# A table of relative biases, spread through a DRAM tape: 16 copies of its rows in place of 128, and eight read-backs in place of one

## The chip, the cores and the metric

The kernel runs on one core of a Trainium2 chip. The metric is the device time of one execution in microseconds (us); lower is better. The engines are TensorE (PE, with its weight loads shown as PEld), VectorE (DVE), ScalarE (ACT), GpSimd (POOL) and SyncE (SP). Each has its own queue of instructions and runs it in order. Transfers are issued by SP (the weights), by POOL (small inputs, and the table of this case) and once by ACT, and run on 16 DMA engines.

## The reference

Two blocks of a network on x of shape (1, 512, 1024), all in fp32. The first is a SwiGLU feed-forward layer, a mixer (chunked attention with 8 heads of 64, beside a pooling of trailing means), and a second feed-forward layer, with RMS norms and residuals. The second block has differential attention, an mLSTM and an MLP. The part that the change touches is the bias of the chunked attention, which depends on the distance of query and key alone, clipped at 128:

```python
x = x + 0.5 * swiglu_ffn(rmsnorm(x, ffn1_norm[l]), ...)
x = x + hybrid_mixer(rmsnorm(x, mix_norm[l]), ...)      # holds chunked_attention
x = x + 0.5 * swiglu_ffn(rmsnorm(x, ffn2_norm[l]), ...)

# chunked_attention: each chunk of 64 attends to itself and the 8 before it
rel_idx = jnp.clip(qpos - kpos, -REL_CLIP, REL_CLIP) + REL_CLIP
bias = rel_bias.astype(jnp.float32)[:, rel_idx]          # rel_bias: (8 heads, 257)
s = jnp.einsum('bhqd,bhkd->bhqk', qb, kb).astype(jnp.float32) * scale + bias
s = jnp.where(valid[None, None], s, NEG_INF)
p = jax.nn.softmax(s, axis=-1)
```

## The kernel before, in words

**Tiles.** Activations stand with features on 128 partitions and the 512 tokens in the columns. Every fp32 operand is split into a high and a low part of a shorter type, and each product is three matmuls (high x high, high x low, low x high). A weight tile of 128 x 1024 words is loaded by SP into one of 3 buffers `wraw`; ScalarE copies its high part to `whi` and VectorE subtracts to get `wlo`, each with 4 buffers. The load of the third tile on is issued when a tile has been split. One weight tile feeds 24 matmuls of 512 columns in the feed-forward layer.

**The first feed-forward layer (`ffn`).** It goes in three chunks of 8, 8 and 6 blocks of 128 hidden features. For each block there are a gate and an up product into two banks; VectorE multiplies both by the norm's scale, ScalarE takes silu of the gate, POOL multiplies the two, and ScalarE and VectorE split the result into its two parts for the down product at the end of the chunk. Behind the second chunk two side jobs are noted: `late_cols` and `toeplitz`.

**The bias table (`toeplitz`).** The biases of the 256 nearest distances, less that of the farthest, are turned around with two small transposes and two small matmuls into a row `rv` of 384 words for each of 8 heads, of which the first 128 are zero. POOL then issues a write of these rows, repeated, to a DRAM tile, the tape, and reads it back with a stride that is one word shorter than a row, so that each partition gets the row shifted by one more word: a table with the same value along each diagonal, `te[128, 8, 512]`, in the memory that held x (`XT`). A POOL memset then masks a part of it (partitions 0 to 63, 64 columns of each head). The table is read by VectorE in the score step of the mixer (`soft_unit`).

**Order.** Nothing is issued as it is written. `Program.note` records each instruction with its operands, a price in ns and, for a transfer, a landing time; `Program.issue` then runs a list schedule in 60 sweeps forwards and backwards, with a little random noise on the ranks (one draw for each noted instruction in each sweep, from a fixed seed), keeps the shortest plan and issues each engine's queue in its order. The first block, up to the end of the mixer, is planned in one go, and the rest in a second. All instructions thus have the line of the issuing loop, 232, and are told apart by their tiles. Of a transfer the planner takes:

```python
if "dma" in fn:
    op.dma = max(math.prod(outs[0].shape) / 90.0, 300.0)
    op.lag = 1900.0 + op.dma
...
if "dma" in fn:
    return {"POOL": 1000.0}.get(eng, 60.0)
```

Of the kernel before, what the change touches and what calls it, by code (L numbers as in the profile page):

```python
# [9 lines left out]
F32 = mybir.dt.float32  # L10
# [5 lines left out]
P = 128  # L16
S = 512
H2 = 256
# [36 lines left out]
class Engine:  # L55
    """Stands for an engine's queue: what is called on it is noted, not issued."""
# [8 lines left out]
class Program:  # L65
    """Notes the instructions in the order of the data flow, then issues each engine's in the order of a list schedule:
    of those whose operands are there, one early in the program or with a long path behind it goes first."""
# [12 lines left out]
    @staticmethod  # L80
    def boxes(aps):
        """(tile, first and end partition, first and end column) of each run."""
        out = []
        for ap in aps:
            t = ap.tensor
            if not isinstance(t, tile.Tile):
                continue
            dims = list(ap.ap)
            if ap.space == bass.MemoryType.DRAM:
                out.append((t.name, 0, 1, 0, 1))  # L90
                continue
            row, parts = dims.pop(0)
            p0, f0 = divmod(ap.offset, row)
            runs = [f0]
            while len(dims) > 1 and len(runs) * dims[0][1] <= 32:
                s, c = dims.pop(0)
                runs = [f + s * i for f in runs for i in range(c)]
            n = sum(s * (c - 1) for s, c in dims) + 1
            out += [(t.name, p0, p0 + parts, f, f + n) for f in runs]
        return out  # L100
# [29 lines left out]
    def edge(self, a, b, flow=True):  # L130
        """b after a; flow: b reads what a writes."""
        if a.dma:
            lat = 60.0
        elif a.eng == b.eng and not flow:
            lat = 0.0
        else:
            lat = SIGNAL[a.eng][b.eng]
        if a.i < self.first:
            b.floor = max(b.floor, a.end + lat)
        else:  # L140
            a.succ[b.i] = max(a.succ.get(b.i, 0.0), lat)

    def table(self, name):
        """Loads a set of function tables, after every use of the one before it."""
        op = self.add("ACT", self.engines[2].queue.preload_act_table_set, (name,), {}, 1290.0)
        for u in self.users + [self.load] * (self.load is not None):
            self.edge(u, op)
        self.load, self.users = op, []
# [30 lines left out]
    @staticmethod  # L179
    def cost(eng, fn, outs, ins, k):  # L180
        """Nanoseconds that the instruction holds its engine."""
        n = max(math.prod(x.shape[1:]) for x in outs[:1] + ins[:1])
        psum = any(x.space == bass.MemoryType.PSUM for x in outs[:1] + ins)
        if "dma" in fn:
            return {"POOL": 1000.0}.get(eng, 60.0)
        if eng == "PE":
            n = math.prod(outs[0].shape[1:])
            if fn == "transpose":
                return max(0.855 * n, 13.0)
            return max(n, 256) / 2.4 + 3 if k["rhs"].dtype == F32R else max(1.667 * n, 214.0)  # L190
        cols = sum(1 for x in ins if math.prod(x.shape[1:]) == 1 and n > 1)
        if eng == "ACT":
            return 0.834 * n + (51.0 if psum else 93.0) + 93.0 * (cols + (k.get("accum_out") is not None))
        if eng == "POOL":
            return 2.11 * n + 147.0 if fn == "tensor_tensor" else 0.83 * n + 200.0
        big = [x for x in ins if math.prod(x.shape[1:]) > 1]
        if len(big) <= 1 and not psum:
            return 0.52 * n + 65.0 + 61.0 * cols
        return 1.041 * n + 69.0 + 61.0 * cols

# [1 line left out]
    def issue(self):  # L202
        """Issues what was noted since the last time. Sweeps forwards and backwards in turn, each by the times of the one
        before with a little noise, and the shortest counts."""
        first, ops = self.first, self.ops[self.first:]
        after = [[(j - first, lat) for j, lat in op.succ.items()] for op in ops]
        before = [[] for _ in ops]
# [27 lines left out]
    def sweep(self, ops, nexts, needs, rank, back):  # L235
# [8 lines left out]
        while n < len(ops):  # L244
# [11 lines left out]
            # one that comes soon and is more urgent is waited for  # L256
# [21 lines left out]
class Arena:  # L278
    """Memory of the phases, cut from one tile for each type."""
# [35 lines left out]
class Kern:  # L315
# [22 lines left out]
    def turn(self, b, blocks):  # L338
        """Transposes of blocks of 128 columns, side by side."""
        for i, x in enumerate(blocks):  # L340
            self.pe.transpose(b[:, i * P:(i + 1) * P], x, self.ident)

    def split(self, h, l, src, g=None):
        """Two parts of src (times the column g) that hold all its bits."""
        if g is None:
            self.act(h, src, AF.Copy)
            self.tt(l, src, h.bitcast(F32), ALU.subtract)
        else:
            self.act(h, src, AF.Copy, scale=g)
            self.stt(l, src, g, h.bitcast(F32), ALU.mult, ALU.subtract)  # L350

    def rsqrt(self, v, n, y, t):
        """y = v ** -0.5 on [128, n] columns."""
        v, y, t = v[:, :n], y[:, :n], t[:, :n]
        self.ts(y.bitcast(I32), v.bitcast(I32), -0.5, ALU.mult, 1597463007.0, ALU.add)
        for _ in range(3):
            self.tt(t, y, y, ALU.mult)
            self.stt(t, t, -0.5, v, ALU.mult, ALU.mult)
            self.stt(y, t, 1.5, y, ALU.add, ALU.mult)

# [112 lines left out]
    def fgroup(self, ps, w, xs, c0=0, cols=slice(0, S)):  # L473
        """Features on partitions: the weights stay, the tokens move."""
        wh, wl = w
        n = len(xs)
        for k in range(n):
            self.mm3(ps, wh[:, k, c0:c0 + P], wl[:, k, c0:c0 + P], xs[k][0][:, cols], xs[k][1][:, cols],
                     k == 0, k == n - 1)

    def fgroups(self, bs, ws, xs, cols=slice(0, S)):
        """The same for several banks, step by step."""
# [5 lines left out]
    def tstep(self, b, w, xs, t, k, start, stop, cols=slice(0, S)):  # L488
        """Tokens on partitions: block t's share of the k-th rows."""
# [16 lines left out]
    def sum_parts(self, b, src, mat, eps, n=S):  # L506
        """b = mat.T @ (src + eps), src in two exact parts."""
# [6 lines left out]
    def rs_wide(self, b, n, y, t, eng=None):  # L514
        """y = (b / n) ** -0.5: a seed from the tables, then a Newton step."""
# [18 lines left out]
    def norm(self):  # L534
        """rsb[:, t] = rms(x[t]) ** -1 on every partition."""
# [4 lines left out]
    def to_cols(self, b, dst, src):  # L540
        """One row of src as a column for each block of tokens."""
# [8 lines left out]
    def setup(self):  # L550
# [6 lines left out]
        self.tape = dp.tile([8, P, 384], F32, name="tape")  # L557
# [63 lines left out]
    def first_norm(self):  # L621
        tb = Rot(self.B[4:8])
        # the clock of the tensor engine rises while it is busy
# [25 lines left out]
    def toeplitz(self, T):  # L649
        """T[q, h, 512 - w + s] = bias of a key s of w, less that of the farthest; later chunks masked."""  # L650
# [14 lines left out]
        self.po.dma_start(self.tape, rv.unsqueeze(1).to_broadcast([8, P, 384]))  # L665
# [3 lines left out]
        self.po.dma_start(te[:, :, H2:], bass.AP(src.tensor, src.offset + P, [[383, P], [384 * P, 8], [1, H2]]))  # L669
        self.po.memset(te[0:64, :, 448:512], NEG)  # L670

# [37 lines left out]
    def stack_q(self, dst, src, half, g=None):  # L709
        """dst = [high part; low part] of the 64 rows of src in the given half."""  # L710
# [8 lines left out]
    def stack_k(self, kh, kl, src, half, g=None):  # L719
        """kh, kl = the high part of the 64 rows, twice, and the low part."""  # L720
# [4 lines left out]
    def qk_mm(self, out, a, b, half):  # L725
        """Of stacked operands (one of them a q, the other kh and kl)."""
# [18 lines left out]
    def transposes(self, E, PT, PL=None):  # L745
        """The blocks of E turned into PT[s, t] for each block of keys."""
# [149 lines left out]
    def prep_final(self, m):  # L896
        """Operands of the second block's first product, and both sums of squares."""
# [12 lines left out]
    def norm_final(self):  # L910
        """The two norms in a row: rsb and rcol for both, X scaled by the first."""
# [26 lines left out]
    def diff_phase(self):  # L938
        I = self.I
        with self.mem.scope() as T:  # L940
# [25 lines left out]
            # gate weights  # L966
# [39 lines left out]
            # lambda  # L1006
# [63 lines left out]
    def gates(self, gs, one, g8):  # L1070
        """Rows of the mLSTM's gates: log of the forget gate, stabiliser, sums within blocks of keys."""
# [144 lines left out]
    def mlp_phase(self):  # L1216
        I = self.I
        X, y = self.X, self.y
        with self.mem.scope() as T:
# [19 lines left out]
            # last part of the mixer's product, then its norm and the residual, by halves of the tokens  # L1239
# [39 lines left out]
            def post(t, cs_, b, part):  # L1279
                """Adds the last part, squares for the norm, and the gain."""  # L1280
# [35 lines left out]
            for t in range(NT):  # L1316
# [9 lines left out]
                # rsqrt(v + eps) of the product's mean square v: a seed from the tables, then a Newton step  # L1326
# [81 lines left out]
```

## Time and profile before

| | |
|---|---|
| median of 3 timed runs | 1563.83 us (1563.27 to 1564.39) |
| profiled execution, first to last instruction | 1561.2 us |
| median less that span | 2.6 us |
| mean granted TensorE clock | 0.993 of full speed |
| TensorE busy | 1531.9 us, 98% of the span |
| VectorE, ScalarE, POOL busy | 53%, 41%, 19% |
| DMA | 142.06 MB, mean 91 GB/s |

The profile gives the span of the profiled execution; no other total stands beside it. A busy share is the part of the span in which an engine works; matmuls are pipelined, so a slow matmul also counts as busy. The granted clock is TensorE's clock as a share of full speed: 1.00 is 2.4 GHz and 0.50 is 1.2 GHz. An arrow in a row names what released the waiting engine last. Names of tiles are written without buffer numbers; `a1f` and `a1r` are the common memory of the first block, of plain fp32 and of split operands.

### The profile page before, as it was taken

The numbers are of one execution on the slowest core, as the hardware profiler recorded it, in microseconds if no ns is written. First come the engines' busy times: TensorE is split into PE (matmuls) and PEld (weight loads), VectorE is DVE, ScalarE is ACT, GpSimd is POOL, SyncE is SP. The second block draws the span as 40 slices with busy tenths as digits, with TensorE's granted clock in tenths as the row PEclk, the third lists the DMA queues.
The fourth block names the chain that finished last, engine by engine and source line by source line (L and its number), as shares of the span: only waits on it lengthen the run. The fifth ranks groups of instructions, "written<-read, shape, count | busy, mean of one in ns | idle before, by whom it ended". The sixth has DMA issues, their size and how long they took to land.

```text
span 1561.2 us, 17985 instructions
## 1 busy us (share of the span) xinstructions
PE 1531.9 (98%) x6931; PEld 1238.2 (79%) x6931; DVE 827.3 (53%) x1284; ACT 647.8 (41%) x1063; POOL 295.4 (19%) x283
## 2 busy tenths in 40 slices
PE   9999999979999999999999999999999999999997
PEld 7888888868867788888888887677778888888886
DVE  6453343335588895433433457988568524344345
ACT  6321231224347763322322355876555534233232
POOL 5120110012054340100200137321106000000002
PEclk9999999989999999999999999999999999999999
DMA  6333333453321114333433233121321332322321
GB/s 190 95 98 93 96 103 96 90 123 108 95 68 50 59 55 122 94 94 95 125 88 102 81 97 101 51 82 32 92 82 44 122 94 90 100 94 94 95 94 54
DMA packets 227237, 142.06 MB, mean 91 GB/s; under 512 B 5524, under 2 KB 212976, under 8 KB 227152
## 3 DMA queue, kind: packets, MB, share of 16 engines
q1 hardware_dynamic: 224832, 136.33, 29.5%
q0 software_dynamic: 2304, 4.59, 1.8%
q8 instruction: 54, 0.88, 0.2%
q14 instruction: 31, 0.25, 0.1%
q10 hardware_dynamic: 16, 0.00, 0.0%
HBM read 137.23 MB, written 3.67 MB: 90 GB/s over the span
## 4 chain that ended last, share of the span: by engine, by line
PE 85%; DVE 6%; issue 3%; DMA 3%; ACT 1%; POOL 1%; SPq 0%; DVEq 0%; POOLq 0%; ACTq 0%
PE bank L232 85%; DMA wraw<-ffn_w_gate 2%; DVE a2f L232 1%; DVE wlo L232 1%; DVE X L232 1%; DVE sq L232 1%; ACT a2f L232 1%; DVE a1r L232 1%; DVE xl L232 0%; POOL a1f L232 0%; DVE a2r L232 0%; DVE XT L232 0%; DMA XT<-x 0%; ACT whi L232 0%; DVE cv L232 0%
## 5 line engine op out<-in xcount | busy, mean ns | idle before, releaser
L232 DVE TENSOR_TENSOR wlo<-wraw,whi 128x1024 fp32r<-128x1024 f32 (+2 forms) x258 | 325.8, 1264 | 449.3 <-ACT whi L232 399.7
L232 ACT ACTIVATE whi<-wraw 128x1024 fp32r<-128x1024 f32 (+2 forms) x258 | 267.3, 1039 | 535.9 <-PE bank L232 493.4
L232 PE MATMUL bank<-xh,whi 128*128 128x512 f32 (+1 forms) x1272 | 464.2, 386 | 10.2 <-ACT whi L232 8.2
L232 PE MATMUL bank<-xl,whi 128*128 128x512 f32 (+1 forms) x1272 | 463.3, 385 | 2.5 <-DVE xl L232 2.5
L232 PE MATMUL bank<-xh,wlo 128*128 128x512 f32 (+1 forms) x1272 | 461.2, 385 | 0.0
L232 PEld LDWEIGHTS bank<-xh,whi 128*128 128x128 f32 x1272 | 239.8, 190 | 59.7 <-ACT whi L232 9.4
L232 PEld LDWEIGHTS bank<-xl,whi 128*128 128x128 f32 x1272 | 240.4, 190 | 50.0 <-DVE xl L232 3.0
L232 PEld LDWEIGHTS bank<-xh,wlo 128*128 128x128 f32 x1272 | 239.8, 190 | 47.5 <-issue 1.4
L232 PE MATMUL bank<-whi,a2r 128*128 128x512 f32 (+1 forms) x528 | 155.6, 388 | 0.0
L232 PE MATMUL bank<-a1r,whi 128*128 128x512 f32 x480 | 149.1, 398 | 0.0
L232 PE MATMUL bank<-a2r,whi 128*128 128x512 f32 x416 | 130.0, 397 | 0.0
L232 PEld LDWEIGHTS bank<-whi,a2r 128*128 128x128 f32 x528 | 98.3, 188 | 21.0
L232 POOL TENSOR_TENSOR a2f<-a2f 128x512 f32<-128x512 f32 x38 | 56.4, 1484 | 303.6 <-DVE a2f L232 252.4
L232 POOL TENSOR_TENSOR a1f<-a1f 128x512 f32<-128x512 f32 x40 | 59.4, 1485 | 248.2 <-DVE a1f L232 234.2
L232 PEld LDWEIGHTS bank<-a1r,whi 128*128 128x128 f32 x480 | 89.3, 188 | 21.5 <-issue 0.6
L232 PE MATMUL bank<-wlo,a2r 128*128 128x512 f32 (+1 forms) x264 | 95.0, 389 | 0.0
L232 PEld LDWEIGHTS bank<-a2r,whi 128*128 128x128 f32 x416 | 77.3, 187 | 19.0 <-issue 0.7
L232 PE MATMUL bank<-a1r,wlo 128*128 128x512 f32 x240 | 91.3, 400 | 0.0
L232 ACT ACTIVATE a2r<-a2f 128x512 fp32r<-128x512 f32 (+3 forms) x83 | 51.0, 620 | 93.1 <-POOL a2f L232 55.3
L232 DVE TENSOR_TENSOR a2r<-a2f,a2r 128x512 fp32r<-128x512 f32 (+2 forms) x81 | 54.8, 679 | 49.7 <-ACT a2r L232 48.9
L232 PE MATMUL bank<-a2r,wlo 128*128 128x512 f32 x208 | 79.4, 397 | 0.0
L232 POOL TENSOR_TENSOR X<-X,a2f 128x512 f32<-128x512 f32 (+1 forms) x9 | 10.7, 1212 | 337.6 <-ACT a2f L232 337.6
(246 smaller groups left out, 1585.7 us busy)
## 6 DMA issues: line engine op xcount, KB each, us to landing
wraw<-ffn_w_gate SPq DMA_DIRECT2D x43, 512.0 KB, 3.7
wraw<-ffn_w_up SPq DMA_DIRECT2D x43, 512.0 KB, 3.7
wraw<-w_in SPq DMA_DIRECT2D x40, 512.0 KB, 3.8
wraw<-ffn_w_down SPq DMA_DIRECT2D x32, 512.0 KB, 3.9
wraw<-w_up SPq DMA_DIRECT2D x32, 512.0 KB, 4.0
wraw<-w_down SPq DMA_DIRECT2D x32, 512.0 KB, 3.6
wraw<-w_out SPq DMA_DIRECT2D x16, 512.0 KB, 3.4
wraw<-ffn_w_down SPq DMA_DIRECT2D x16, 384.0 KB, 3.4
```

The lines of the kernel that those rows point to most:

```text
L232: op.fn(*op.a, **op.k)
```

## The change

The tape holds each head's row 16 times in place of 128 times. One shifted read of it can then fill 16 partitions only, so the read-back is done in eight transfers of 16 partitions each, each starting 16 words earlier in the row than the one before. The rest of the computation is the same. The file after also lacks the comments and docstrings of the one before, with empty lines in their place.

```diff
-        self.tape = dp.tile([8, P, 384], F32, name="tape")
+        self.tape = dp.tile([8, 16, 384], F32, name="tape")
...
-        self.po.dma_start(self.tape, rv.unsqueeze(1).to_broadcast([8, P, 384]))
+        self.po.dma_start(self.tape, rv.unsqueeze(1).to_broadcast([8, 16, 384]))
         self.T = te = self.XT[:].rearrange("p t d -> p (t d)").rearrange("p (h c) -> p h c", h=8)
         self.po.memset(te[:, :, :H2], 0.0)
         src = self.tape[:]
-        self.po.dma_start(te[:, :, H2:], bass.AP(src.tensor, src.offset + P, [[383, P], [384 * P, 8], [1, H2]]))
+        for a in range(8):
+            self.po.dma_start(te[16 * a:16 * a + 16, :, H2:],
+                              bass.AP(src.tensor, src.offset + P - 16 * a, [[383, 16], [384 * 16, 8], [1, H2]]))
         self.po.memset(te[0:64, :, 448:512], NEG)
```

## Rows read from the trace of the kernel before

**Rows 1.** The page: span, busy time, and two lines of the 40 slices (tenths).

```profile
span 1561.2 us, 17985 instructions
...
PE 1531.9 (98%) x6931; PEld 1238.2 (79%) x6931; DVE 827.3 (53%) x1284; ACT 647.8 (41%) x1063; POOL 295.4 (19%) x283
...
PE   9999999979999999999999999999999999999997
...
PEclk9999999989999999999999999999999999999999
```

**Rows 2.** Windows of 40 us: length, busy time (instructions), clock, DMA share, GB/s.

```profile
280.00:320.00 40.00, 40.00 (x178) 32.38 (x177) 11.07 (x15) 6.03 (x7) 2.41 (x2) 1.00 0.47 75
320.00:360.00 40.00, 31.75 (x120) 24.27 (x119) 16.80 (x19) 12.96 (x17) 9.12 (x8) 0.87 0.48 130
```

**Rows 3.** Finer windows, busy by PE, PEld, DVE, ACT, POOL; the last is their whole.

```profile
308.00:312.00 4.00, 4.00 (x19) 3.30 (x19) 0.00 (x0) 0.00 (x0) 0.00 (x0) 1.00 0.51 55
322.90:328.20 5.30, 0.10 (x2) 0.04 (x1) 0.06 (x1) 1.06 (x1) 0.96 (x1) 0.93 0.66 160
328.20:334.10 5.90, 5.82 (x12) 3.60 (x12) 1.16 (x1) 0.00 (x0) 0.96 (x2) 0.50 1.01 303
334.10:337.10 3.00, 0.04 (x1) 0.04 (x1) 0.75 (x2) 2.18 (x4) 0.78 (x1) 0.96 0.01 4
337.10:341.30 4.20, 4.20 (x11) 3.07 (x12) 4.10 (x5) 0.98 (x2) 2.13 (x1) 0.59 0.33 98
322.90:341.30 18.40, 10.15 (x24) 6.75 (x24) 6.08 (x7) 4.22 (x6) 4.83 (x4) 0.72 0.59 166
```

**Rows 4.** TensorE's waits over the whole span: us in total, times, longest.

```profile
PE bank L232 <- ACT whi L232: 8.2, 2, 5.2
```

**Rows 5.** The chain of waits, 292 to 338 us: start, us, what.

```profile
292.54 34.05 DMA wraw<-ffn_w_gate
326.64 0.96 POOL XT L232
...
333.66 1.24 POOL a1f L232
...
337.06 51.33 PE bank L232 x214
```

**Rows 6.** DMA issues of the whole span: count, KB each, median us to landing.

```profile
wraw<-ffn_w_gate SPq DMA_DIRECT2D x43, 512.0 KB, 3.7
...
tape<-a1f POOLq DMA_DIRECT2D x1, 1536.0 KB, 34.9
...
XT<-tape POOLq DMA_DIRECT2D x1, 1024.0 KB, 6.4
...
rows<-mix_norm POOLq DMA_DIRECT2D x1, 4.0 KB, 3.8
```

**Rows 7.** DMA issues from 280 to 345 us alone.

```profile
wraw<-ffn_w_gate SPq DMA_DIRECT2D x3, 512.0 KB, 24.8
```

**Rows 8.** Timeline of POOL from 291 us: start, duration, what, idle before.

```profile
291.21 1.14 POOL L232 DMA_DIRECT2D tape<-a1f  x1 [55.74 <-issue]
293.27 1.28 POOL L232 TENSOR_TENSOR a1f<-a1f 128x512 f32<-128x512 f32 x1 [0.93 <-DVE a1f L232]
```

**Rows 9.** Timeline of ScalarE, 327 to 338 us.

```profile
327.05 1.06 ACT L232 ACTIVATE whi<-wraw 128x1024 fp32r<-128x1024 f32 x1 [23.12 <-DMA wraw<-ffn_w_gate]
...
335.97 1.99 ACT L232 ACTIVATE whi<-wraw 128x1024 fp32r<-128x1024 f32 x2
```

**Rows 10.** Timeline of POOL, small loads: first and last of nine, and `k_rcnt`.

```profile
1.68 0.71 POOL L232 DMA_DIRECT2D rows<-mix_norm  x1
...
5.87 0.49 POOL L232 DMA_DIRECT2D rows<-conv_w  x1
...
196.59 0.54 POOL L232 DMA_DIRECT2D a1f<-k_rcnt  x1
```

**Rows 11.** Timeline of VectorE: the table's first reader.

```profile
455.59 0.68 DVE L232 CUSTOM_DVE_ANT_0 a1f<-bank,XT 128x512 f32<-128x512 f32 x1
```

## The prediction

> **What bounds the kernel now.** I read the page's slices first. TensorE is busy in nearly every slice at the full granted clock; of the 40 slices, the ninth is the only one in the middle of the span where both digits fall [rows 1]. So time can only be won or lost where TensorE stops or slows. The 40 us windows put the dip at 320 to 360 us: 120 matmuls against 178 in the window before, with a granted clock of 0.87 [rows 2]. At 40 / 178 = 0.225 us a matmul, 58 missing ones are 13.0 us.
>
> Finer windows show its parts [rows 3]. From 322.9 to 341.3 us, 18.4 us, TensorE did 24 matmuls, which need 24 x 0.225 = 5.4 us: again 13.0 us lost. There are two holes, about 5.2 and 3.0 us (8.2 in all, and the waits name ScalarE's weight split `whi` for both [rows 4]). The other 4.8 us are slow matmuls: after the first hole the granted clock is 0.50, that is 1.2 in place of 2.4 GHz, for 5.9 us, and after the second it is 0.59 over 4.2 us.
>
> Then the chain of waits, for what stands behind `whi` [rows 5]. It goes back from TensorE's start at 337.06 us through a product of POOL's, what POOL does in the table's memory, its issue of the read-back at 326.64 us, and a 34.05 us transfer. The chain calls that one `wraw<-ffn_w_gate`, but POOL's read-back can only be waiting for the tape. The DMA issues settle it [rows 6]: the tape's write of 1536 KB took 34.9 us to land, from an issue at 291.21 us [rows 8]; it landed at 326.1, just before POOL issued the read-back. The weight load beside it was dragged along: three gate loads in this stretch have a median of 24.8 us, against 3.7 us for all 43 [rows 6, 7]. While the write runs almost alone (308 to 312 us) the 16 DMA engines are 0.51 busy and move 55 GB/s [rows 3]: about half of them work, each full, and a weight load that needs all 16 queues behind that half.
>
> So two stalls have one cause. First: the load issued at 292.54 us is late, its split starts at 327.05 us after a 23.1 us wait for DMA [rows 9], and TensorE starts again as that split ends. Second: POOL, in order, stands at the read-back from the end of its product at 293.27 us, then at the mask until 333.66 us [rows 5, 8]. The SwiGLU product behind it comes late, ScalarE's two-part split of that product waits for it, and the weight splits at 335.97 us stand behind that split on ScalarE [rows 9]; TensorE resumes at 337.06 us [rows 5].
>
> **The change, part by part.**
>
> *Tape write, 128 copies to 16.* 1536 KB become 192 KB. By bytes alone 34.9 / 8 = 4.4 us; a small POOL load with next to no bytes, `rows<-mix_norm`, took 3.8 us [rows 6], so fixed part plus bytes is at most 3.8 + 4.4 = 8.2 us. I take 6. The leading dimension stays 8, so half of the engines again. POOL's issue of 1024 runs took 1.14 us [rows 8]; 128 runs cost about what the 128-partition `k_rcnt` load cost, 0.54 us [rows 10].
>
> *The weight load beside it.* Issued at 292.54 us, landing in 3.7 us, it would be there at 296.2. TensorE ran out at 322.9, and a split takes 1.1 us, so a start by 321.8 us costs nothing: cover 25.6 us. The delay by the small write is at most its 8.2 us. First stall: gone.
>
> *Read-back, one transfer to eight.* The bytes stay 1024 KB in 1024 runs. POOL issues eight instructions in place of one of 0.96 us [rows 5]. Rows for 128 runs or fewer say 0.49 to 0.71 us each, most near 0.5 [rows 10]; the bound from above is the old one's 0.96. So 4.0 to 7.7 us, taken as 4.4. The trace has no transfer onto 16 partitions. Below: they overlap, and the last lands about 4 us after its issue, like the other small ones. Above: each takes the 6.4 us of the whole 1024 KB [rows 6], one after the other, 51 us. I take the lower end, because POOL issued nine row loads from 1.68 to 5.87 us, (5.87 - 1.68) / 8 = 0.52 us apart [rows 10], while the first took 3.8 us to land [rows 6]: they were in flight together.
>
> A rule speaks against this part. The Trainium skill, "DMA: Bandwidth & Descriptors", section "Anatomy of one DMA — SWDGE (gpsimd) path", gives each transfer a fixed 2.0 us plus its bytes at 436 GB/s, and "Rules for kernel authors" says to merge small ones and that transfers to separate parts of the partitions serialise. By it, as an estimate, eight reads of 128 KB are 8 x 2.3 = 18.4 us one after another; the row loads above agree with the fixed part in size, but not with its standing in line.
>
> *POOL's hold.* From the write's issue to the end of the mask it was 333.66 - 291.21 = 42.5 us. After: 0.5 (issue) + 6 (write) + 4.4 (issues) + 4 (last landing) + 0.5 (mask) = 15.4 us, so until 306.6. What is needed? With weights on time TensorE would go on at 322.9 for one more tile of 24 matmuls, 5.4 us, to 328.3. From POOL's release to TensorE's start there were 337.06 - 333.66 = 3.4 us [rows 5], so a release by 324.9, a hold of 33.7 us, costs nothing. Second stall: gone, with 18 us to spare. (By the Trainium skill's 18.4 us the hold would be 0.5 + 6 + 18.4 + 0.5 = 25.4 us and still covered, so the sum is the same by both.) Without this cover each us of hold would be a us of TensorE.
>
> *The other users.* The first reader of the table is VectorE's score step at 455.59 us [rows 11], over 120 us later; that it now waits for eight transfers instead of one is hidden there. POOL gains 8 x 0.54 - 0.96 - 0.60 = 2.8 us of work and is 19% busy [rows 1]. The planner prices a POOL transfer at 1000 ns of issue and its landing at 1900 ns plus elements / 90 ns (at least 300). Tape plus read-back is 1.0 + 1.9 + 4.4 + 0.1 + 1.0 + 1.9 + 2.9 = 13.2 us in its plan before, and 1.0 + 1.9 + 0.5 + 0.1 + 8.0 + 1.9 + 0.4 = 13.8 us after. The place in the plan should stay much the same.
>
> *The order of everything.* Seven more noted instructions shift the planner's random draws for all that is noted later, so the order of the first block may change everywhere. Its price has no row. TensorE's idle time outside this stretch is 1561.2 - 1531.9 - 8.2 = 21 us [rows 1, 3], with the start and the end of the span in it; that is all a luckier order can win, and a stretch as bad as this one costs 13. I take 0, with 3 us to either side.
>
> *Sum.* 13.0 us of loss go; nothing comes on the path. The profiled span of 1561.2 us becomes 1548.2. The median of the timed runs is 2.6 us above the span; with that kept, 1563.8 - 13.0 = 1550.8 us.
>
> **The rivals.**
>
> *1. Only the first stall goes.* Either the eight issues or a new order leaves POOL's product, and the weight splits behind it, late. Price kept: the second hole of 3.0 us, and 4.2 - 11 x 0.225 = 1.7 us of slow matmuls behind it [rows 3], 4.7 in all; won 8.3; 1555.5 us. For it: ScalarE's order puts the weight split behind the split of the product. Against: the hold is half of what the cover allows.
>
> *2. Slower: the eight reads stand in line.* If each takes 6.4 us [rows 6] the hold is 0.5 + 6 + 51 + 0.5 = 58 us, to 349 us, and TensorE waits from 328.3 to 352.6, 24 us, plus the clock's loss, 4.8 us as before: 29 in place of 13, so 1580 us. It decides from the point where the hold is again 42.5 us, that is at (42.5 - 7) / 8 = 4.4 us for each read. For it: a transfer with few rows outermost used half of the engines. Against: 16 rows are outermost now, and the row loads overlapped.
>
> *3. The change doesn't remove the stall.* If the weight load is late by itself, the time stays at 1563.8. For it: the chain names that load. Against: the same kind of load takes 3.7 us elsewhere, and the engines are half busy for as long as the tape is written.
>
> *4. A new order costs elsewhere what is won here.* A place as bad as this one gives 1564; a worse one is slower, 1568.
>
> **How the numbers follow.** The full gain: 0.72, with its own range 1547.5 to 1554. Rival 1: 0.13. Rival 2: 0.04. Rival 3: 0.04. Rival 4: 0.07, half of it no change and half slower. Beyond 0.2% (3.1 us, about what a measurement of this kernel can tell from no change) faster is 0.72 + 0.13 = 0.85; within it 0.04 + 0.03 = 0.07; slower 0.04 + 0.04 = 0.08. The likeliest case gives 1550.8 us. The range takes in the order's 3 us below it and rival 1 above it, 1547 to 1557; outside it I leave rivals 2, 3 and 4, 0.15, and the tails of the order.
>
> **What would show it.** Right: the ninth slice full with the clock at full speed; a tape write of 4.4 to 8.2 us; gate loads in this stretch near 4 us; POOL's eight reads about 0.5 us each; the wait for `whi` gone from TensorE's waits; some 178 matmuls in every 40 us around 320. Wrong: reads that land over 4.4 us apart, POOL's mask still ending 40 us after the tape's issue, or a hole of TensorE in another place of the first 560 us, by a new order.

## The result, and the profile after

The changed kernel takes 1547.14 us (median of 4 runs, 1546.74 to 1548.09) against 1563.56 us for the kernel before beside it: a ratio of 0.9894, 95% interval 0.9880 to 0.9908. It is 16.4 us faster; forecast were 13.0 us, and 1550.8 us with a range from 1547 to 1557, so the result lies at the range's lower edge. A second set of runs on another occasion gave 1548.14 against 1562.54 us, 14.4 us, a ratio of 0.9904 (0.9890 to 0.9919).

The page of the changed kernel: span, busy time, two lines of the slices.

```profile
span 1545.2 us, 18001 instructions
...
PE 1525.7 (99%) x6931; PEld 1235.2 (80%) x6931; DVE 824.6 (53%) x1284; ACT 648.4 (42%) x1063; POOL 297.7 (19%) x290
...
PE   9999999999999999999999999999999999999997
...
PEclk9999999999999999999999999999999999999999
```

The ninth slice is full and at full clock, where [rows 1] showed 7 and 8. The same two 40 us windows as in [rows 2]:

```profile
280.00:320.00 40.00, 40.00 (x178) 32.10 (x177) 13.41 (x19) 10.22 (x12) 9.18 (x13) 1.00 0.57 119
320.00:360.00 40.00, 40.00 (x176) 32.74 (x175) 18.93 (x24) 15.02 (x22) 6.32 (x6) 1.00 0.29 84
```

176 matmuls stand in the second window, against 120. The DMA issues from 280 to 345 us, to set beside [rows 6, 7]:

```profile
wraw<-ffn_w_gate SPq DMA_DIRECT2D x3, 512.0 KB, 3.8
...
XT<-tape POOLq DMA_DIRECT2D x8, 128.0 KB, 7.0
tape<-a1f POOLq DMA_DIRECT2D x1, 192.0 KB, 5.7
```

The write lands in 5.7 us in place of 34.9, and the gate loads beside it in 3.8 in place of 24.8. POOL's timeline, against [rows 5, 8]:

```profile
292.89 0.67 POOL L232 DMA_DIRECT2D tape<-a1f  x1
299.14 3.69 POOL L232 DMA_DIRECT2D XT<-tape  x7 [5.58 <-PE bank L232]
304.97 1.28 POOL L232 TENSOR_TENSOR a1f<-a1f 128x512 f32<-128x512 f32 x1 [2.14 <-DVE a1f L232]
306.20 0.55 POOL L232 DMA_DIRECT2D XT<-tape  x1
307.61 0.52 POOL L232 MEMSET XT<- 64x512 f32 x1 [0.85 <-DMA XT<-tape]
```

From the write's issue to the end of the mask 307.61 + 0.52 - 292.89 = 15.2 us pass on POOL, where it was 42.5 us; in the new order a product of POOL's, with a wait of 2.14 us before it, lies in between. The release before the first read-back is again named wrongly (a TensorE bank): what ends there is the wait for the tape. TensorE's waits no longer have a row for `whi`, which [rows 4] showed with 8.2 us.

### The profile page after: what moved, and what is told of

It reads as the page before. It is cut to its first block, busy times and chain, and to the rows that moved or that the text cites. A ratio compares the mean times of both kernels' runs of the same rounds, so it can differ in the third digit from the quotient of the medians.

```text
span 1545.2 us, 18001 instructions
## 1 busy us (share of the span) xinstructions
PE 1525.7 (99%) x6931; PEld 1235.2 (80%) x6931; DVE 824.6 (53%) x1284; ACT 648.4 (42%) x1063; POOL 297.7 (19%) x290
## 4 chain that ended last, share of the span: by engine, by line
PE 92%; DVE 6%; ACT 1%; POOL 0%; issue 0%; DMA 0%; SPq 0%; DVEq 0%; POOLq 0%; ACTq 0%
PE bank L232 92%; DVE a2f L232 1%; DVE wlo L232 1%; ACT a2f L232 1%; DVE X L232 1%; DVE a2r L232 0%; DVE XT L232 0%; DVE xl L232 0%; DVE a1r L232 0%; DVE sq L232 0%; DMA XT<-x 0%; DVE cv L232 0%; POOL a2f L232 0%; DVE acc L232 0%; POOL acc L232 0%
```

## The experiments

To say where the us are, I counted TensorE's work in each trace: for each matmul the median spacing of its width to the next one (0.227 us for 512 columns, 0.272 for 384, 0.120 for 256, 0.109 for 128), summed in the recorded order. The time between two points of this sum, less the sum, is time lost there. The points are 0, 40, 280, 400, 500 and the end, 1473 us of work; the tape's stretch lies in the column 280-400 (from about 292 us of the span on), the mixer in 400-500. The time before the first matmul and behind the last, some 11 us in all, stands in no column.

```
us lost at work of            0-40   40-280  280-400  400-500  500-end   span
before                        7.24     2.98    14.83    12.51    38.61  1561.2
before_again                  6.03     2.95    14.98    12.51    38.66  1560.1
old_order_8reads              6.13     2.97    18.69    12.51    38.65  1563.9
old_order_small               4.88     2.98     1.51    12.49    38.63  1545.5
old_order_small_2             5.78     2.98     1.51    14.12    38.56  1547.9
wide128                       4.95     2.65     1.50    12.54    38.69  1545.4
changed kernel                5.97     3.24     0.93    11.25    38.86  1545.2
after_again                   5.63     3.24     0.93    11.25    38.90  1545.0
copies64                      6.87     3.22     0.93    12.75    38.88  1547.7
copies96                      7.53     3.24     5.62    11.26    38.88  1551.5
new_order_big                 5.34     3.24    13.77    11.24    38.82  1557.4
new_order_as_before           6.48     3.24    11.50    11.25    38.90  1556.4
seed2                         5.86     3.57     0.94    15.31    48.79  1559.2
seed3                         6.95     3.55     1.26    11.05    41.11  1549.9
```

My theory after the result: the write's size made a stall worth 13.3 us, and the new order of the instructions gave the rest. Rivals: A, the small transfers give all of it; B, the order does.

**Sizes and order apart (4 kernels).** The noted instructions and their prices are kept, so that the plan stays, and only what is issued in their place changes. `old_order_small`, in the old order:

```diff
-        self.tape = dp.tile([8, P, 384], F32, name="tape")
+        self.tape = dp.tile([8, 16, 384], F32, name="tape")
...
-        self.po.dma_start(self.tape, rv.unsqueeze(1).to_broadcast([8, P, 384]))
+        self.po.dma_start(self.tape, rv.unsqueeze(1).to_broadcast([8, 16, 384]))
+        op = self.prog.ops[-1]                 # priced as 128 copies
+        op.dma = 8 * 128 * 384 / 90.0
+        op.lag = 1900.0 + op.dma
...
+        self.prog.ops[-1].fn = parts           # issues the eight reads in the place of the one
```

> Every engine's queue in the order of the kernel before; only the tape holds 16 copies and the read-back is issued as eight transfers in the place of the one. Theory (the size of the tape's write made the stall, worth 13.3 us; the new order is worth the other 2.7 us, at the start of the span and around 420 us): 1563.5 - 13.3 = 1550.2 us, between 1549.2 and 1551.2, with no TensorE hole near 322 us. Rival A (the small transfers give the whole gain): 1547.1 us. Rival B (the new order gives the gain, the sizes do not): 1563.5 us.

Measured: 1548.09 us, ratio 0.9904 (0.9889 to 0.9919), 15.2 us below the runs before beside it. That is below the theory's 1549.2 to 1551.2 and nearer to rival A. No wait for `whi` is left. The lost time says how much of the 15.2 us is the stretch: 14.83 - 1.51 = 13.3 us. Another 2.4 us of difference between the two profiles stand in the first 40 us of work, where the two kernels issue the same instructions in the same order; see below.

`old_order_8reads` keeps the 128 copies (`parts` alone).

> The order of the kernel before and its tape of 128 copies; only the read-back is split into eight transfers of 16 partitions. Theory (the write alone makes the stall): 1563.5 us within 1 us, the tape's write again near 35 us and both TensorE holes there. Rival (the one big read-back, which fills all 16 DMA engines, makes the second hole): 4.7 us less, 1558.8 us.

Measured: 1566.12 us, ratio 1.0016 (1.0006 to 1.0025): 2.8 us slower, by the interval 0.9 to 3.9. The rival fell, and the theory's "within 1 us" too: by itself the split is a loss. Where POOL's hold is not covered it is longer by the split: from the read's first issue to the mask 335.73 - 325.56 = 10.2 us passed here, and 6.4 us with the single read in `before_again` (331.93 - 325.52).

`new_order_big` is the changed kernel with 128 copies (and the price of 16):

```diff
-        self.tape = dp.tile([8, 16, 384], F32, name="tape")
+        self.tape = dp.tile([8, 128, 384], F32, name="tape")
...
+        op.dma = 8 * 16 * 384 / 90.0           # priced as 16 copies; the reads' stride is 384 * 128
...
```

> Every queue in the order of the changed kernel and its eight read-backs; only the tape is written 128 times again (the planner is given the price of 16 copies, so that the order stays). Theory: the stall is back, 1547.1 + 13.3 = 1560.4 us, between 1558.5 and 1562.5, with the write near 35 us. Rival B (the order gives the gain): 1547.1 us. Rival A: 1563.5 us.

Measured: 1560.25 us, ratio 0.9981 (0.9972 to 0.9991). The stall is back; in this order too the tape's write decides. The three loads of `ffn_w_up` beside it have a median of 28.4 us, where the changed kernel has 6.5.

`new_order_as_before` has the new order with the old transfers: 128 copies, and the first of the eight noted reads issues the whole read, the others nothing.

> The order of the changed kernel with the transfers of the kernel before: 128 copies, one read-back in the place of the first of the eight. It measures the new order by itself. Theory: 2.7 us less than before, 1560.8 us, and within 1 us of the run with 128 copies and eight read-backs. Rival A (the order is worth nothing): 1563.5 us. Rival B: 1547.1 us.

Measured: 1558.11 us, ratio 0.9964 (0.9953 to 0.9976), 5.2 us less than before, and 2.1 less than with eight reads. More than the theory gave: the new order also shortens the stall, from 14.83 to 11.50 us of lost time. In that order a SwiGLU product of POOL's stands between the read-back and the mask and does not wait for the read. Its line, TensorE's only hole in this stretch, and the window behind the hole:

```profile
329.81 1.28 POOL L232 TENSOR_TENSOR a1f<-a1f 128x512 f32<-128x512 f32 x1
333.27 0.79 PE L232 MATMUL bank<-xh,whi 128*128 128x512 f32 x1 [8.31 <-ACT whi L232]
333.27:337.50 4.23, 4.23 (x10) 3.22 (x11) 3.54 (x4) 1.01 (x2) 1.94 (x2) 0.50 0.60 183
```

TensorE starts 2.2 us after that product ends, while the mask ends only at 335.9 us. In `new_order_big` and `copies96` (below) it again starts 2.2 us after the product and before the mask ends, and in the kernel before, where the product stands behind the mask, TensorE's second start comes 2.2 us after it as well (334.88 and 337.06). So one hole of 8.3 us stands in place of two of 8.2 together, and what is saved is work at half clock: 4.2 us behind the one hole, where [rows 3] had 5.9 us at 0.50 and 4.2 us at 0.59.

**Another execution, and another way to make the write fast (2 kernels).**

> The kernel before, unchanged, for a second profile. Theory now: the time lost around 322 us and in the first 30 us differs between executions of one program, because the moments at which the granted clock goes to full and back differ; the first profile lost 13.3 us in the stretch. Expected here: the same two holes, between 13 and 17 us lost in the stretch. Rival (a program loses the same in each execution): 13.3 us within 0.3.

Measured: 1561.88 us, in one run. The stretch lost 14.98 us against 14.83, or 13.5 against 13.3 above the 1.51 that stay: the rival was right, it repeats. What differs is the start, 6.03 against 7.24 us. In all 14 profiles this first part lies between 4.9 and 7.5 us, in either order. The windows from 0 to 30 us of `before_again` and, below it, of `old_order_small`:

```profile
0.00:30.00 30.00, 26.31 (x119) 21.63 (x120) 17.25 (x21) 20.30 (x32) 19.17 (x28) 0.94 0.76 203
```

```profile
0.00:30.00 30.00, 26.56 (x124) 21.39 (x125) 17.83 (x22) 21.03 (x33) 20.27 (x29) 1.00 0.79 211
```

Busy for the same time, TensorE got 119 matmuls done in the one and 124 in the other, and the granted clock has fallen in the first. The first profile of the kernel before had 114, though its window shows 1.00: a window shows this too where the trace has no record of the clock yet. The last rise to full speed in the start is recorded at 7.5 us in `old_order_small`, which lost least, at 12.5 in `before_again`, 13.5 in the first profile and 14.6 in `copies96`, which lost most; there, matmuls of 512 columns start 0.43 us apart just before the rise and 0.23 us after it.

`wide128` keeps 128 copies, the single read and the old order, but the rows stand on 128 partitions before they are written:

```diff
-        self.ve.tensor_copy(eT, b[:, :16].rearrange("p (i h) -> p i h", i=2))
+        self.ve.tensor_copy(eT, b[:, :16].rearrange("p (i h) -> p i h", i=2)
+                                .unsqueeze(3).to_broadcast([P, 2, 8, 16]))
...
-        self.po.dma_start(self.tape, rv.unsqueeze(1).to_broadcast([8, P, 384]))
+        self.po.dma_start(self.tape.rearrange("h (r c) w -> (h r) c w", r=16),
+                          rv.unsqueeze(1).to_broadcast([P, 8, 384]))
```

> The order, the 128 copies and the single read-back of the kernel before; only the rows are first made on 128 partitions (16 copies by a matmul with 16 times repeated columns), and each partition writes 8 of the 128 copies. The 1536 KB stay. Theory (the write is slow because it comes from 8 partitions and so runs on half of the DMA engines, at a few GB/s each): the write lands in 5 to 12 us, the stall is gone, 1547 to 1549 us. Rival (1536 KB written to the tape are slow from wherever they come): the write near 35 us and 1563.3 us. Between: a write of 17 us, half of 35 with twice the engines, and still no stall, 1548 us.

Measured: 1548.30 us, ratio 0.9904 (0.9889 to 0.9919). The tape's write among its DMA issues, and a window while it runs:

```profile
tape<-a1f POOLq DMA_DIRECT2D x1, 1536.0 KB, 7.3
```

```profile
290.00:295.00 5.00, 5.00 (x23) 4.13 (x22) 1.23 (x2) 0.63 (x1) 1.28 (x1) 1.00 0.92 300
```

The same 1536 KB land in 7.3 us, with the engines 0.92 busy where [rows 3] showed 0.51. So 1536 KB by themselves make no stall; written from 8 partitions they do. The edit changes two things at once, the source partitions and the outermost dimension of the transfer (8 in the one, 128 in the other), and no run tells these apart. The queue of POOL's transfers (packets, MB, share of the 16 engines' time) while the write is on its way, from 291.2 to 326.1 us in the kernel before and, below it, from 288.9 to 296.4 us here:

```profile
q0 software_dynamic: 704, 1.58, 44.9%
```

```profile
q0 software_dynamic: 368, 1.57, 66.3%
```

For the same bytes the packets took 0.449 x 16 x 34.9 = 251 us of engine time in the one and 0.663 x 16 x 7.5 = 80 us in the other.

**The cover (2 kernels).** The changed kernel with 64 and with 96 copies, the planner's price kept:

```diff
-        self.tape = dp.tile([8, 16, 384], F32, name="tape")
+        self.tape = dp.tile([8, 64, 384], F32, name="tape")      # 96 in the other
...
```

> The order and the eight read-backs of the changed kernel, with 64 copies in the tape in place of 16. The cover that the prediction worked out is 25.6 us for the weight load and a hold of POOL of 33.7 us. Theory: a write of about 18 us and a hold of 28 us are covered, 1547.1 us within 1.5. Rival (the loss grows in proportion to the copies, 12 us by 112 copies): 1547.1 + 5 = 1552.4 us.

Measured: 1546.59 us, ratio 0.9893 (0.9876 to 0.9909). The write took 18.1 us, POOL's hold 28.7 us (293.78 to 322.46), and no `whi` stands in TensorE's waits: hidden, as the theory had it.

> As the run with 64 copies, with 96. Theory: a write of 26 to 27 us and a hold of 36 to 37 us are just past the cover, so one short hole of TensorE, and with it some us at half clock: 1549 to 1553 us. Rival (in proportion): 1547.1 + 9 = 1556.1 us.

Measured: 1551.00 us, ratio 0.9925 (0.9910 to 0.9940). The write took 26.4 us, the hold 39.9 us (294.46 to 334.31), 3 us more than expected. TensorE's waits of this run have one for `whi`, and the window shows it:

```profile
PE bank L232 <- ACT whi L232: 2.6, 1, 2.6
```

```profile
320.00:360.00 40.00, 37.36 (x156) 29.90 (x155) 17.89 (x22) 15.13 (x21) 11.64 (x16) 0.96 0.56 128
```

Not in proportion to the copies: nothing up to 64, then 4.7 us of lost time (5.62 - 0.93) at 96, of which 2.6 are the hole and the rest slow matmuls.

The hold up to the mask is not what decides in this order, though, for TensorE waits for the product ahead of the mask. From the tape's issue to the end of that product 23.7 us passed with 64 copies, 32.0 with 96, 37.7 in `new_order_as_before` and 40.5 in `new_order_big`; the hole for `whi` was 0, 2.6, 8.3 and 11.2 us. Each of the three holes is the time beyond 29.4 us: this is the cover in the new order.

**What an order is worth (4 kernels).**

> The changed kernel, unchanged, beside the next run on the same chip. Theory: the new order is worth 1.6 us between 400 and 500 us (the profiles: 0.76 to 1.0 us of lead gained there over the old order with the same small transfers), so this run is 1.6 us, between 0.8 and 2.4, below the run of the old order. Rival (the order is worth nothing, and the 3.4 us beyond the forecast are the difference between executions): the two agree within 0.5 us.

> The old order with the small tape and the eight read-backs, a second time, with more rounds. Theory: 13.3 us (the stall alone) below the runs of the kernel before, ratio 0.9915, and 1.6 us above the changed kernel. Rival: 15 us below, ratio 0.990, and level with the changed kernel.

Measured on the same chip: 1548.14 us (0.9904, 0.9890 to 0.9919) in the new order and 1548.94 us (0.9908, 0.9893 to 0.9923) in the old one. The timed difference of 0.8 us, where 1.6 were expected, is inside both intervals and decides nothing. The traces do: in the mixer the old order loses 12.49 to 12.54 us in five of its six profiles, and the new one 11.24 to 11.26 us in five of six. The sixth of each has 1.5 to 1.6 us more, a dip of the clock. The window from 440 to 460 us of `old_order_small_2`, and of `old_order_small` below:

```profile
440.00:460.00 20.00, 19.03 (x76) 13.81 (x77) 13.78 (x33) 9.41 (x19) 5.38 (x6) 0.91 0.17 52
```

```profile
440.00:460.00 20.00, 19.95 (x86) 14.59 (x86) 14.48 (x34) 11.61 (x24) 5.55 (x6) 1.00 0.17 53
```

Then the planner's draws from other seeds, one line of the changed kernel:

```diff
-        rng = random.Random(1)
+        rng = random.Random(2)                 # 3 in the other
```

> The changed kernel with the planner's random draws from another seed, so that every queue of both blocks has another order. It sizes what an order alone is worth. Theory (with all stalls of the tape gone, orders differ by what they leave idle in the stretches that VectorE bounds): within 3 us of the changed kernel, 1544 to 1550 us. Rival (an order can cost as much as the tape's stall): over 1553 us.

> As the run with the second seed, with a third: 1544 to 1550 us by the theory, over 1553 us by the rival.

Measured: 1561.19 us, ratio 0.9989 (0.9979 to 0.9998), and 1551.75 us, 0.9928 (0.9913 to 0.9943). Against `after_again` beside them the two are 13.1 and 3.6 us slower. Both are outside the theory's range of 1544 to 1550 us, and seed 2 is where the rival had it, over 1553: with a fast tape, an order alone loses 9.9 us more behind the mixer (48.79 against 38.86) and 4.1 in the mixer. The windows of seed 2 from 880 us on:

```profile
880.00:960.00 80.00, 76.01 (x320) 60.65 (x319) 49.47 (x50) 40.17 (x58) 38.73 (x26) 0.96 0.34 94
960.00:1040.00 80.00, 75.61 (x344) 57.16 (x343) 66.87 (x145) 57.08 (x117) 23.56 (x22) 0.97 0.20 53
```

TensorE has holes there, and the clock falls in them. No kernel tried is clearly below the changed one: `copies64` and `wide128` agree with it.

## Why the prediction was right in mechanism and short in size

**Tape write.** 6 us were taken, between 4.4 and 8.2; it took 5.7. That half of the engines were busy was read rightly from 0.51, but that was not all: from 128 partitions the same bytes landed faster by 34.9 / 7.3 = 4.8. The Trainium skill, "DMA: Bandwidth & Descriptors", "Why a DMA increments its semaphore by 16 and not by 1", says that a transfer runs on the largest number of engines up to 16 that divides the slowest dimension of both sides; with 8 rows outermost that is 8, and the trace's 0.51 agrees. It explains a factor of 2. The rest is in the packets, which took 251 / 80 = 3.1 times as much engine time from 8 partitions: on 8 engines 251 / 8 = 31.4 of the 34.9 us, on 16 engines 80 / 16 = 5.0 of the 7.3. Why they took longer, no run here shows.

**The weight load and TensorE's first hole.** Gone; gate loads at 3.8 us. That the tape drags the loads along is shown by two pairs that differ in the number of copies alone, with the same order and the same eight reads: the gate loads take a median of 28.3 us in `old_order_8reads` and 6.7 in `old_order_small`, the up loads 28.4 in `new_order_big` and 6.5 in the changed kernel. The times follow: 1566.12 against 1548.09 us, 1560.25 against 1547.14.

**Eight reads.** 0.53 us each, seven in 3.69 us, as forecast at 0.54. From the first issue to the mask 307.61 - 299.14 = 8.5 us passed, where 8.4 were forecast, but this agreement is luck. The forecast let the mask wait for all eight reads, the last landing 4 us after its issue. The mask writes partitions 0 to 63 alone, and in every trace with eight reads it starts 0.1 us after the fourth has landed. The last, issued at 306.20 us, took 7.2 us:

```profile
XT<-tape POOLq DMA_DIRECT2D x1, 128.0 KB, 7.2
```

All eight had landed 14.3 us after the first issue (in `old_order_small`, with no product of POOL's between, 12.8 us), against 6.4 us for the one read. They overlap, but not as much as was forecast; the table's first reader, 120 us later, hides it. The Trainium skill's figure for eight in a row ("DMA: Bandwidth & Descriptors", an estimate), 18.4 us, is not what the trace shows either, and the 3.8 us of the row loads were nearly twice the fixed part of 2.0 us with which the prediction let them agree.

**POOL's hold.** 15.4 us forecast, 15.2 measured: the write's part was right (299.14 - 292.89 = 6.2 us for 6.5), the reads' part came out by the luck just told. The cover of 33.7 us up to the mask was worked out for the old order, and no run tests it there; that it lies between the holds of `copies64` (28.7, free) and `copies96` (39.9, not free) says little, since in their order the product ahead of the mask decides, with a cover of 29.4 us. That without cover a us of hold is a us of TensorE is borne out in the old order by the reads alone: 10.2 - 6.4 = 3.8 us longer, 18.69 - 14.98 = 3.7 us more lost. In the new order it holds for the product (the three holes above) and not for the mask.

**The sum.** 13.0 us were forecast for the stretch; with the order kept it is 14.83 - 1.51 = 13.3. Right. The step that failed is the last term of the sum, the one for the order, which was put at nothing for want of a row: "I take 0, with 3 us to either side". In the traces it gave (14.83 - 13.3 - 0.93) + (12.51 - 11.25) + (2.98 - 3.24) + (38.61 - 38.86) = 0.6 + 1.3 - 0.3 - 0.2 = 1.4 us. And the forecast was made on one execution: its start happened to lose 7.24 us, and that of the first profile after 5.97, 1.3 us that belong to no kernel (in the old order the start lost 4.88 to 7.24 us, in the new one 5.34 to 7.53). Together 13.3 + 1.4 + 1.3 = 16.0 us, the difference of the spans, 1561.2 - 1545.2. Of the timed differences, 16.4 and 14.4 us, 14.7 are thus explained by the kernel; the rest, up to 1.7 us, is as large as executions of one kernel differ (1547.06 to 1549.42 us in the second set) and is given no other cause.

**The rivals.** The second hole staying (1) did not come. Reads in line (2) came in a small form: the split costs 2.8 and 2.1 us where nothing covers it. The change not doing what it says (3) is refuted by `new_order_big`. A costly new order (4) was this time a small gain; `seed2` shows that the 0.07 given to it, with 3 us to either side otherwise, was too sure: one of two other orders lost 13 us (1561.19 against 1548.14 beside it).

## What to carry to other kernels

Look where TensorE stops first, then at what lands late there: a transfer that nobody needs for 120 us can still hold up the weights, and the queue of the engine that waits for it. Spread a write's source over all partitions before making it smaller; both took the stall away here. Work out the cover for the instruction that is waited for in the order that will run: behind the mask and ahead of it are two different covers. An agreement of a sum is no proof of its terms, as the 8.5 us for the reads show. If a planner with random draws orders the instructions, keep the order fixed to measure a change, or the order's own worth, from 1 to 13 us here, is counted with it.

## What the runs showed that I had not expected

The start loses 4.9 to 7.2 us with the same instructions in the same order (old order, six profiles), by the moment at which the granted clock reaches full, recorded between 7.5 and 13.5 us; and a dip of the clock around 440 us, worth 1.5 to 1.6 us, came in one of six profiles of either order. A write of 1536 KB from 8 partitions moved 45 GB/s (1.57 MB in 34.9 us) and from 128 partitions 215 GB/s (in 7.3 us), landing included. From 8 partitions the landing grows in step with the bytes: 5.7, 18.1, 26.4 and 34.9 us for 192, 768, 1152 and 1536 KB, so 29.2 us for 1344 KB more, 47 GB/s.
